# Normalising the softmax weights on POOL, and the small parts of the streamed weights on DVE, in a two-layer diffusion backbone

## The chip, the cores and the metric

One core of one Trainium2 chip runs the whole program in one launch. The metric is the device time of the launch in microseconds (us), lower is better. A difference under about 0.3% (6.4 us here) can't be told from no change.

The engines are named as the profile names them: PE (TensorE, matmuls and transposes), PEld (its weight loads), DVE (VectorE), ACT (ScalarE), POOL (GpSimd) and SP (SyncE, which here does nothing but issue DMAs; its issuing time stands under SPq). Each engine works through its own instructions in program order; engines wait for each other by semaphores. All tensors live in SBUF tiles of 128 partitions; matmul results come out in PSUM tiles of 128x512.

## The reference, cut to what matters

Two layers over 256 latent tokens (a grid of 4 rows by 64) and 256 context tokens, width 1024, fp32. A layer is a SwiGLU half step, a mixer and another SwiGLU half step. The change lies in the mixer, whose three branches are a neighbourhood attention (8 heads of 64), a Fourier mixing and a windowed attention (8 query heads, 2 key heads, a sink logit per head). Layer 0 also attends from the context tokens; layer 1, the last, doesn't.

```python
def neighbourhood_attention(q, k, v, kc, vc, bias_tab, rows):
    ...
    s_loc = jnp.where(in_win[:, :, None, :], s_loc, NEG_INF)
    ...
    p = jax.nn.softmax(jnp.concatenate([s_loc, s_ctx], axis=-1), axis=-1).astype(v.dtype)
    ...
def window_gqa_attention(q, k, v, kc, vc, sink):
    ...
    p = jax.nn.softmax(jnp.concatenate([s_loc, s_ctx, s_sink], axis=-1), axis=-1).astype(v.dtype)
    ...
def reference(...):
    h, hc = x, ctx
    for l in range(DEPTH):
        ...
        nq, nk, nv, fu, wq, wk, wv, gl = split_projection(u @ w_in[l])
        ...
        h = h + gt2 * merge_branches(a, f, w, gl, w_br[l], w_out[l])
```

## The kernel before

**The streamed weights.** Every projection runs over weights that come from HBM in 424 sub-tiles of 128x1024 (512 KB each, eight 128x128 blocks). The class `Weights` (L43 to L101) streams them. A product keeps fp32 accuracy by three matmuls per block, in `mm3` (L292 to L297): large part of the weight with large and small part of the activations (L295, L296), small part of the weight with the large part (L297). So each raw sub-tile is loaded by SP (L58), copied to its large part `wh` by ACT (L67), and its small part `wl` = raw minus `wh` is made at L76 by the engine in `lo_engine`. That engine is DVE, except at a few stretches where it is POOL; the two attention stretches (set by two lines in `mix`, L1056 and L1058) hold 18 sub-tiles in layer 0 and 22 in layer 1. `next` hands out the blocks. At the first block of sub-tile n it issues what is still missing of the `wl` of n, the `wh` of n+1 and the loads; at the fifth block the `wl` of n+1. The pool of raw tiles has 3 buffers, and a load waits until the `wl` three sub-tiles before has read its buffer.

**The attention.** 16 blocks in layer 0 and 8 in layer 1 (a block is a pair of heads over 256 queries) run through a software pipeline written out in `attention` (L720 to L848), with four steps per block. Step by step: two score matmuls (L733, L734) give a 128x512 tile of scores (128x256 for context queries). DVE adds the mask and takes the row's extreme (L740), ACT takes the exponential and its sum (L742; L745 for the sink). `normalise` takes two tiles at a time, tiles 0 and 1 of the block and two steps later tiles 2 and 3: DVE adds the sinks (L753), takes the reciprocals (L755) and scales both tiles (L759). Then PE transposes the weights chunk by chunk over all four tiles (L764), ACT copies the large part (L766), DVE makes the small part (L771), and PE multiplies with the values (L782). At a block's end ACT copies the result out (L788) and POOL adds its halves (`gather`, L794). Between the steps `fill` runs pieces of the projections that are due (queries, keys, gates) by a table of due times, `DUES`. It is these pieces that pull weights through `next`.

**The other users of the queues.** Projected keys and queries are stacked into operand tiles by DMAs from SBUF to SBUF that SP issues (`stack`, L891): four for a query, eight for a key. SP also issues the raw loads (L58) and the loads of the bias table (L714), all in program order. The rotary embedding runs on POOL (L913), and its small part is made on DVE (L918); `turn` copies the projected values on ACT (L935) and transposes them on PE (L939).

**The tiles.** Activations, scores and temporaries share one pool, `act_p`, of N_ACT tiles of 128x512. A tile's next writer waits for the last reader of what it held before, DMAs included.

Of the kernel before, what the change touches and what calls it, by code (L numbers as in the profile page):

```python
# [10 lines left out]
ALU = mybir.AluOpType  # L11
# [20 lines left out]
NEG = -1e30  # L32
SUB = 8
N_SUB = 424
N_ACT = 70
TAIL = 3
FOLD = (1, 2, 3)
EARLY_GATES = 6, 12
# [4 lines left out]
class Weights:  # L43


    def __init__(self, nc, src, raw_p, w_p):
        self.nc, self.src, self.raw_p, self.w_p = nc, src, raw_p, w_p
        self.order, self.pos = [], 0
        self.loaded = self.n_hi = self.n_lo = 0
        self.raw, self.hi, self.lo = {}, {}, {}  # L50
        self.on_tile = None
        self.lo_engine = nc.vector
        self.ahead = 1
# [30 lines left out]
    def next(self, key, width=1):  # L84
        n, o = divmod(self.pos, SUB)
        assert o + width <= SUB
        if o == 0:
            self.hi.pop(n - 1, None)
            self.lo.pop(n - 1, None)
            self.lo_to(n + 1)  # L90
            self.hi_to(n + 1 + self.ahead)
            self.load_to(self.n_lo + 3)
        elif o == SUB // 2:
            self.lo_to(n + 1 + self.ahead)
        if self.on_tile and o % self.tile_step == 2:
            self.on_tile()
        self.order.append((key, width))
        self.pos += width
        s = slice(o * 128, (o + width) * 128)
        return self.hi[n][:, s], self.lo[n][:, s]  # L100
# [165 lines left out]
class Emit:  # L266
    def __init__(self, ctx, tc, d):
        self.tc, self.nc, self.d = tc, tc.nc, d
        pool = lambda name, bufs, **k: ctx.enter_context(tc.tile_pool(name=name, bufs=bufs, **k))
        self.const = pool("const", 1)  # L270
        self.act_p = pool("act", N_ACT)
        self.raw_p = pool("raw", 3)
        self.w_p = pool("w", 6)
        self.mod_p = pool("mod", 2)
        self.sm_p = pool("sm", 4)
        self.ps_p = pool("ps", 8, space=PSUM)
        self.W = Weights(self.nc, d["ws"], self.raw_p, self.w_p)
        self.mod = {}
# [90 lines left out]
    def setup(self):  # L369
# [15 lines left out]
        self.first_w = {}  # L385
        loads = self.first_loads(0), self.first_loads(1)
        next(loads[0])
        self.h = [c.tile([128, NT], F32, name=f"h{k}") for k in range(KD)]
        for k in range(KD):
# [18 lines left out]
        for _ in range(KD // 2):  # L408
            next(scale)
        for k in range(KD):  # L410
            self.stat(k, 0, NT, True)
        norm = Norm(self, 0, 0, NT, self.first_shift)
        next(scale, None)
        norm.stage1(0, 1)
        self.first_shift(0)
# [304 lines left out]
    def attention(self, makers, fill):  # L720
# [3 lines left out]
        nc = self.nc  # L724
# [23 lines left out]
        def normalise(b, i0, i1):  # L748

            nk = len(b["kc"]) * 128  # L750
            r, s = b["r"][:, i0:i1], b["sum"][:, i0:i1]
            if b["sink"] is not None:
                nc.vector.tensor_tensor(out=s, in0=s, in1=b["es"][:, i0:i1], op=ALU.add)  # L753
                yield
            nc.vector.reciprocal(out=r, in_=s)  # L755
            yield
            for i in range(i0, i1):
                e = b["p"][i][:, :nk]
                nc.vector.tensor_scalar(out=e, in0=e, scalar1=b["r"][:, i:i + 1], scalar2=None, op0=ALU.mult)  # L759

        def transposes(b, c):
            ps = self.ps()
# [44 lines left out]
        for g in range(4 * len(makers) + 8):  # L807
            if g % 4 == 0 and g // 4 < len(makers):
                b = makers[g // 4]()
# [7 lines left out]
            for i in range(2):  # L817
                y = at(g, 3 + 2 * i, 1)
                if y:
                    norms.append(normalise(y[0], 2 * i, 2 * i + 2))  # L820
# [13 lines left out]
            for i in range(max(0, g // 4 - 4), len(blocks)):  # L834
                b = blocks[i]
# [15 lines left out]
    def mix(self, l, norm, nxt):  # L851
        nc, W = self.nc, self.W
# [200 lines left out]
        fill(0.0)  # L1053
        pieces(4)
        f = next(fourier)
        W.lo_engine = nc.gpsimd  # L1056
        self.attention(makers, fill)
        W.lo_engine = nc.vector  # L1058
        while pending or later:
            pieces(1, True)  # L1060
        early = [ready(("gate", i)) for i in range(n_early)]
# [175 lines left out]
```

## Time and profile before

| | us |
|---|---|
| median of 3 runs | 2136.06 |
| lowest and highest | 2133.22 and 2138.77 |
| the profiled execution | 2132.6 |
| its span, first to last instruction | 2130.8 |
| PE busy | 2058.0 (97%) |
| DVE busy | 1310.0 (61%) |
| ACT busy | 853.6 (40%) |
| POOL busy | 436.4 (20%) |

The busy share of an engine is an average over the whole span, in which the stages differ. The attention of layer 0 lies at about 500 to 680 us, that of layer 1 at about 1690 to 1840 us. In a row of the waits, the first name is the instruction that waited, the arrow points to what released it, and then stand total us, times, and the longest. In a row of the timeline the columns are start, length, engine, line, operation, tiles written and read, shape and count, and in brackets how long the engine sat idle before it and what ended that.

### The profile page before, as it was taken

To read this page: it belongs to the slowest core of one execution; us is meant where nothing else is said; L and a number is where in the kernel's file an instruction comes from. 1 tells how busy PE (TensorE), PEld (TensorE's weight loads), DVE (VectorE), ACT (ScalarE), POOL (GpSimd) and SP (SyncE) were. 2 spreads that over 40 slices of the span, in tenths; PEclk is the share of its full clock that TensorE was granted. 3 is DMA by queue.
4 is the path that set the end of the run, shared out by engine and by line. 5 is a ranking of instruction groups with operands and counts; after the bars stand their busy time and mean duration, and the time that the engine had idled before them with its cause. 6 is when DMAs were issued, how large, how long until landed. Compare 5 with 4: busy or idle time off the path is not lost. (4 is left out here: it accounts for less than half of the span.)

```text
span 2130.8 us, 29228 instructions
## 1 busy us (share of the span) xinstructions
PE 2058.0 (97%) x11193; PEld 1771.7 (83%) x11193; DVE 1310.0 (61%) x2074; ACT 853.6 (40%) x1362; POOL 436.4 (20%) x318
## 2 busy tenths in 40 slices
PE   7899999999999999999999999999999989999998
PEld 3788888878888888888888888888888878999998
DVE  6777776565676334777777575533337548566554
ACT  4422222345787223432222243222324458645443
POOL 4200000433542112600000140000024155332002
PEclk8999999999999999999999999999999999999999
DMA  6455556445522323455656545623334563555664
GB/s 250 138 198 187 192 194 212 138 120 151 137 82 80 96 93 99 134 181 192 195 187 201 198 145 189 195 92 99 99 116 139 145 170 113 150 179 157 182 183 131
DMA packets 119412, 327.05 MB, mean 153 GB/s; under 512 B 30692, under 2 KB 35940, under 8 KB 119272
## 3 DMA queue, kind: packets, MB, share of 16 engines
q1 hardware_dynamic: 119272, 325.18, 49.0%
q8 instruction: 88, 1.44, 0.3%
q14 instruction: 52, 0.43, 0.1%
HBM read 305.99 MB, written 1.05 MB: 144 GB/s over the span
## 5 line engine op out<-in xcount | busy, mean ns | idle before, releaser
L296 PE MATMUL ps<-act,wh 128*128 128x512 f32 (+1 forms) x3227 | 1122.3, 348 | 23.8 <-DVE act L220 11.7
L295 PE MATMUL ps<-act,wh 128*128 128x512 f32 (+1 forms) x3227 | 1122.8, 348 | 2.1 <-ACT act L208 1.1
L297 PE MATMUL ps<-act,wl 128*128 128x512 f32 (+1 forms) x3227 | 1120.6, 347 | 0.8 <-DVE wl L76 0.8
L67 ACT ACTIVATE wh<-raw 128x1024 fp32r<-128x1024 f32 x424 | 447.5, 1057 | 749.7 <-PE ps L296 596.6
L296 PEld LDWEIGHTS ps<-act,wh 128*128 128x128 f32 x3227 | 614.6, 190 | 100.5 <-DVE act L220 14.2
L295 PEld LDWEIGHTS ps<-act,wh 128*128 128x128 f32 x3227 | 614.5, 190 | 77.8 <-ACT act L208 1.3
L297 PEld LDWEIGHTS ps<-act,wl 128*128 128x128 f32 x3227 | 614.6, 190 | 76.2 <-DVE wl L76 1.1
L76 DVE TENSOR_TENSOR wl<-raw,wh 128x1024 fp32r<-128x1024 f32 x346 | 432.9, 1253 | 254.7 <-ACT wh L67 254.3
L317 DVE CUSTOM_DVE_ANT_0 dump<-ada,silu_row 128x1024 bf16<-128x1024 f32 x224 | 273.5, 1221 | 11.4 <-DMA ada<-in_w_ada 9.1
L76 POOL TENSOR_TENSOR wl<-raw,wh 128x1024 fp32r<-128x1024 f32 x78 | 190.9, 2450 | 239.4 <-ACT wh L67 226.2
L304 ACT ACTIVATE act<-tmp 128x512 fp32r<-128x512 f32 (+1 forms) x122 | 66.8, 566 | 268.5 <-DVE tmp L522 255.0
L460 POOL TENSOR_TENSOR tmp<-h 128x512 f32<-128x512 f32 (+1 forms) x7 | 11.6, 1660 | 737.0 <-DVE h L477 592.7
L477 DVE SCALAR_TENSOR_TENSOR h<-ps,mod,h 128x256 f32<-128x256 f32 x136 | 61.7, 481 | 150.9 <-PE ps L297 150.9
L522 DVE TENSOR_TENSOR tmp<-tmp,ps 128x512 f32<-128x512 f32 (+1 forms) x88 | 54.6, 621 | 113.6 <-PE ps L297 107.7
L305 DVE TENSOR_TENSOR act<-tmp,act 128x512 fp32r<-128x512 f32 (+1 forms) x122 | 74.3, 626 | 61.2 <-ACT act L304 61.2
L771 DVE TENSOR_TENSOR act<-ps,act 128x512 fp32r<-128x512 f32 x80 | 54.9, 686 | 33.5 <-ACT act L766 33.2
L466 POOL TENSOR_TENSOR tmp<-h 128x256 f32<-128x256 f32 (+1 forms) x44 | 51.6, 1174 | 116.3 <-DVE h L477 98.4
L742 ACT ACTIVATE tmp<-tmp,sm 128x512 f32<-128x512 f32 (+1 forms) x96 | 62.1, 647 | 29.1 <-DVE sm L740 27.4
L782 PE MATMUL ps<-act 128*128 128x256 f32 x320 | 63.1, 310 | 9.2 <-DVE act L771 8.0
L450 POOL MEMSET tmp<- 128x256 f32 x16 | 4.8, 312 | 308.5 <-PE ps L297 307.8
L766 ACT ACTIVATE act<-ps 128x512 fp32r<-128x512 f32 x80 | 47.5, 593 | 36.4 <-PE ps L764 35.9
L1101 DVE TENSOR_TENSOR tmp<-tmp,ps 128x512 f32<-128x512 f32 (+1 forms) x48 | 26.0, 551 | 54.3 <-PE ps L297 53.0
(111 smaller groups left out, 1479.5 us busy)
## 6 DMA issues: line engine op xcount, KB each, us to landing
raw<-in_ws SPq DMA_DIRECT2D x424, 512.0 KB, 3.7
ada<-in_w_ada SPq DMA_DIRECT2D x128, 512.0 KB, 3.7
act<-act SPq DMA_DIRECT2D x112, 128.0 KB, 2.3
tmp<-in_w_ada_sc SPq DMA_DIRECT2D x16, 256.0 KB, 5.4
tmp<-in_w_ada SPq DMA_DIRECT2D x16, 256.0 KB, 6.0
tmp<-in_na_bias SPq DMA_DIRECT2D x64, 64.0 KB, 2.7
h<-in_h SPq DMA_DIRECT2D x8, 256.0 KB, 5.6
act<-act SPq DMA_DIRECT2D x32, 64.0 KB, 2.0
```

The lines of the kernel that those rows point to most:

```text
L67: self.nc.scalar.activation(out=wh, in_=self.raw[i], func=AF.Copy)
L76: self.lo_engine.tensor_tensor(out=wl, in0=self.raw.pop(i), in1=self.hi[i].bitcast(F32), op=ALU.subtract)
L295: mm(ps, lhsT=w[0], rhs=x[0], start=start, stop=False)
L296: mm(ps, lhsT=w[0], rhs=x[1], start=False, stop=False)
L297: mm(ps, lhsT=w[1], rhs=x[0], start=False, stop=stop)
L304: nc.scalar.activation(out=hi, in_=src, func=AF.Copy)
L305: nc.vector.tensor_tensor(out=lo, in0=src, in1=hi.bitcast(F32), op=ALU.subtract)
L317: self.nc.vector.tensor_tensor_reduce(out=self.dump[:, ks], in0=w, in1=self.silu_row[:, v, ks], scale=1.0, scalar=m if half else 0.0, op0= ...
L477: self.nc.vector.scalar_tensor_tensor(out=h, in0=ps, scalar=self.mod[l, g][:, v, j:j + 1], in1=h, op0=ALU.mult, op1=ALU.add)
L742: nc.scalar.activation(out=e[:, :nk], in_=e[:, :nk], func=AF.Exp, scale=-1.0, bias=nm, accum_out=b["sum"][:, i:i + 1])
L771: nc.vector.tensor_tensor(out=t[1], in0=ps, in1=t[0].bitcast(F32), op=ALU.subtract)
L782: nc.tensor.matmul(b["ps"][hp][:, :256], lhsT=v, rhs=t[j][:, cs], start=c == 0 and j == 0, stop=c == n - 1 and j == 1)
```

## The change

`normalise` scales on POOL instead of DVE: 64 operations on 128x512 and 32 on 128x256 in all. The two assignments of `lo_engine` around the attention go, so 40 of the small parts are made on DVE that were made on POOL. The raw pool has 5 buffers for 3, and `next` issues the loads two sub-tiles further ahead. The pool of activation tiles has 66 tiles for 70.

```diff
-N_ACT = 70
+N_ACT = 66
...
-            self.load_to(self.n_lo + 3)
+            self.load_to(self.n_lo + 5)
...
-        self.raw_p = pool("raw", 3)
+        self.raw_p = pool("raw", 5)
...
             for i in range(i0, i1):
                 e = b["p"][i][:, :nk]
-                nc.vector.tensor_scalar(out=e, in0=e, scalar1=b["r"][:, i:i + 1], scalar2=None, op0=ALU.mult)
+                nc.gpsimd.tensor_scalar(out=e, in0=e, scalar1=b["r"][:, i:i + 1], scalar2=None, op0=ALU.mult)
...
         f = next(fourier)
-        W.lo_engine = nc.gpsimd
         self.attention(makers, fill)
-        W.lo_engine = nc.vector
```

Three places show how the instructions move. The first is POOL in the windowed attention of layer 0. Before, between the rotary products (L913) and the sums at a block's end (L794) stand small parts of weights (L76):

```order
L913 TENSOR_TENSOR tmp<-tmp,cos 128x256
L913 TENSOR_TENSOR tmp<-tmp,sin 128x256
L913 TENSOR_TENSOR tmp<-tmp 128x256
L794 TENSOR_TENSOR tmp<-tmp 128x256
L76 TENSOR_TENSOR wl<-raw,wh 128x1024
L794 TENSOR_TENSOR tmp<-tmp 128x256
L76 TENSOR_TENSOR wl<-raw,wh 128x1024
```

In the changed kernel the same place holds the scalings (L759), each pair behind one of the sums:

```order
L913 TENSOR_TENSOR tmp<-tmp,cos 128x256
L913 TENSOR_TENSOR tmp<-tmp,sin 128x256
L913 TENSOR_TENSOR tmp<-tmp 128x256
L794 TENSOR_TENSOR tmp<-tmp 128x256
L759 TENSOR_SCALAR tmp<-tmp,sm 128x512 x2
L794 TENSOR_TENSOR tmp<-tmp 128x256
L759 TENSOR_SCALAR tmp<-tmp,sm 128x512 x2
L759 TENSOR_SCALAR tmp<-tmp,sm 128x256 x4
```

The small parts have left POOL, and the second pair of scalings of a latent block now stands behind an L794.

The second place is DVE in the same stretch, around the small part of a rotated query (L918) and the small part of the transposed softmax weights (L771). Before:

```order
L755 RECIPROCAL sm<-sm 128x2
L759 TENSOR_SCALAR tmp<-tmp,sm 128x512 x2
L740 ISA tmp,sm<-ps,wa_mask,nsink 128x512
L740 ISA sm 128x1
L918 SCALAR_TENSOR_TENSOR act<-tmp,act 128x512
L771 TENSOR_TENSOR act<-ps,act 128x512
L740 ISA tmp,sm<-ps,wa_mask,nsink 128x256
```

And in the changed kernel:

```order
L755 RECIPROCAL sm<-sm 128x2
L740 ISA tmp,sm<-ps,wa_mask,nsink 128x512
L740 ISA sm 128x1
L918 SCALAR_TENSOR_TENSOR act<-tmp,act 128x512
L76 TENSOR_TENSOR wl<-raw,wh 128x1024
L771 TENSOR_TENSOR act<-ps,act 128x512
L740 ISA tmp,sm<-ps,wa_mask,nsink 128x256
```

A small part of weights (L76) now stands between L918 and L771, and the two scalings ahead of L740 are gone.

The third place is DVE in layer 1, where the last keys and queries of the neighbourhood attention are evacuated (L898). The names in brackets are semaphores that the instruction waits for; those that begin with DMA belong to transfers. Before:

```order
L898 SCALAR_TENSOR_TENSOR act<-ps,act 128x256 [waits DMAHW3_49,Activation_49]
L755 RECIPROCAL sm<-sm 128x2
L771 TENSOR_TENSOR act<-ps,act 128x512 [waits DMAHW2_49,DMAHW1_49,DMAHW3_49,DMAHW0_49,PE_49]
L759 TENSOR_SCALAR tmp<-tmp,sm 128x512 [waits DVE_49]
L759 TENSOR_SCALAR tmp<-tmp,sm 128x512
L740 ISA tmp,sm<-ps,tmp 128x512 [waits DMAHW0_49,DMAHW5_49,PE_49,Pool_49]
```

And in the changed kernel, from the same L898:

```order
L898 SCALAR_TENSOR_TENSOR act<-ps,act 128x256 [waits DMAHW0_49,DMAHW1_49,DVE_49,Activation_49]
L76 TENSOR_TENSOR wl<-raw,wh 128x1024 [waits Activation_49]
L76 TENSOR_TENSOR wl<-raw,wh 128x1024 [waits DVE_49,DMAHW5_49,PE_49,Activation_49]
L76 TENSOR_TENSOR wl<-raw,wh 128x1024 [waits DVE_49,DMAHW6_49,PE_49,Activation_49]
L755 RECIPROCAL sm<-sm 128x2
L771 TENSOR_TENSOR act<-ps,act 128x512 [waits DMAHW2_49,DMAHW3_49,DMAHW1_49,DMAHW0_49]
L740 ISA tmp,sm<-ps,tmp 128x512 [waits DMAHW4_49,DMAHW5_49,DVE_49,DMAHW7_49,PE_49,Pool_49]
```

Three small parts stand between L898 and L771 now. With 66 tiles for 70, L898, L771 and L740 write tiles that other transfers have read than before: in the changed kernel's program, L898 takes the tile that the last of the four moves issued from 1711.81 us reads, L771 one that the fifth to the eighth of the twelve moves issued from 1715.88 us read, and L740 one that the last of these twelve reads.

## Rows read from the trace of the kernel before

**Rows 1.** The busy times by stretch. Columns: the stretch in us from the span's start and its length, then the busy us of PE, PEld, DVE, ACT and POOL with the count of instructions, PE's mean granted clock as a share of full speed, the DMA engines' busy share and GB/s.

```profile
500.00:680.00 180.00, 174.37 (x969) 147.63 (x968) 123.85 (x311) 134.44 (x328) 73.85 (x60) 1.00 0.40 105
1723.00:1730.50 7.50, 0.36 (x4) 0.15 (x2) 0.91 (x3) 2.73 (x5) 2.66 (x2) 0.66 0.88 276
1730.50:1737.00 6.50, 6.50 (x31) 5.88 (x31) 0.87 (x3) 2.63 (x5) 5.72 (x6) 0.60 0.54 124
```

**Rows 2.** The waits between 500 and 680 us (attention of layer 0), those of PE.

```profile
PE ps L782 <- DVE act L771: 2.2, 7, 0.3
PE ps L733 <- DMA act<-act: 2.2, 1, 2.2
```

**Rows 3.** The waits between 1700 and 1840 us (attention of layer 1), those of ACT for raw weights and the longest of PE.

```profile
ACT wh L67 <- DMA raw<-in_ws: 19.1, 4, 8.6
PE ps L939 <- ACT tmp L935: 7.1, 1, 7.1
PE ps L782 <- DVE act L771: 5.8, 6, 1.9
```

**Rows 4.** The timeline of layer 1 around 1710 to 1731 us: ACT, PE, SP, DVE.

```profile
1720.44 1.06 ACT L67 ACTIVATE wh<-raw 128x1024 fp32r<-128x1024 f32 x1 [8.64 <-DMA raw<-in_ws]
1729.10 0.71 ACT L742 ACTIVATE tmp<-tmp,sm 128x512 f32<-128x512 f32 x1
...
1722.58 0.72 PE L782 MATMUL ps<-act 128*128 128x256 f32 x4
1730.44 0.90 PE L939 MATMUL ps<-ident,tmp 128*128 128x128 f32 x3 [7.14 <-ACT tmp L935]
...
1711.81 2.47 SPq L891 DMA_DIRECT2D act<-act  x4
1715.88 7.78 SPq L891 DMA_DIRECT2D act<-act  x12
...
1710.89 0.42 DVE L898 SCALAR_TENSOR_TENSOR act<-ps,act 128x256 fp32r<-128x256 f32 x1 [1.20 <-ACT act L896]
1722.52 0.69 DVE L740 CUSTOM_DVE_ANT_0 tmp<-ps,tmp 128x512 f32<-128x512 f32 x1 [7.56 <-PE ps L734]
```

**Rows 5.** The page's list of DMA issues: the moves from tile to tile, with the median us from issue to landing at the end of the row.

```profile
act<-act SPq DMA_DIRECT2D x112, 128.0 KB, 2.3
```

**Rows 6.** Groups of instructions on POOL over the whole span: after the shape the count, then busy us and mean ns of one, then the idle time before them.

```profile
L450 POOL MEMSET tmp<- 128x256 f32 x16 | 4.8, 312 | 308.5 <-PE ps L297 307.8
L441 POOL TENSOR_SCALAR nsink<-sink 128x32 f32<-128x32 f32 x1 | 0.3, 339 | 0.0
```

**Rows 7.** All operations of three lines over the whole span: count, shortest, median and longest in ns, first and last start, shapes. L1104 adds two tiles, L76 makes a small part of weights, L753 adds the sinks.

```profile
L1104 POOL TENSOR_TENSOR tmp<-tmp x14: 735/1292/2207, 679.2 to 1892.9; 128x512 f32<-128x512 f32 x7, 128x256 f32<-128x256 f32 x7
...
L76 DVE TENSOR_TENSOR wl<-raw,wh x346: 1212/1223/2335, 83.2 to 2113.3; 128x1024 fp32r<-128x1024 f32 x173
L76 POOL TENSOR_TENSOR wl<-raw,wh x78: 2342/2401/2900, 24.4 to 1940.4; 128x1024 fp32r<-128x1024 f32 x78
...
L753 DVE TENSOR_TENSOR sm<-sm x24: 148/156/1773, 593.3 to 1810.7; 128x2 f32<-128x2 f32 x24
```

**Rows 8.** The scalings L759 of 128x512, first those between 500 and 680 us, then those between 1720 and 1840 us.

```profile
L759 DVE TENSOR_SCALAR tmp<-tmp,sm 128x512 f32<-128x512 f32 x32 | 18.9, 634 | 0.5
...
L759 DVE TENSOR_SCALAR tmp<-tmp,sm 128x512 f32<-128x512 f32 x26 | 18.9, 766 | 0.3
```

**Rows 9.** The timeline at five places in the attention of layer 0: first POOL's operation behind which the second pair of scalings of a block stands in the changed order, then PE's four transposes (L764) of that block's first chunk.

```profile
580.76 0.80 POOL L913 TENSOR_TENSOR tmp<-tmp 128x256 f32<-128x256 f32 x1
582.21 0.60 PE L764 MATMUL ps<-ident,tmp 128*128 128x128 f32 x4
...
600.94 0.74 POOL L794 TENSOR_TENSOR tmp<-tmp 128x256 f32<-128x256 f32 x1 [1.12 <-ACT tmp L788]
601.92 0.60 PE L764 MATMUL ps<-ident,tmp 128*128 128x128 f32 x4
...
620.68 0.74 POOL L794 TENSOR_TENSOR tmp<-tmp 128x256 f32<-128x256 f32 x1 [1.11 <-ACT tmp L788]
621.69 0.60 PE L764 MATMUL ps<-ident,tmp 128*128 128x128 f32 x4
...
640.71 0.73 POOL L794 TENSOR_TENSOR tmp<-tmp 128x256 f32<-128x256 f32 x1 [1.72 <-ACT tmp L788]
640.18 0.93 PE L764 MATMUL ps<-ident,tmp 128*128 128x128 f32 x4
...
657.29 0.81 POOL L794 TENSOR_TENSOR tmp<-tmp 128x256 f32<-128x256 f32 x1 [0.92 <-ACT tmp L788]
657.61 0.60 PE L764 MATMUL ps<-ident,tmp 128*128 128x128 f32 x4
```

**Rows 10.** The timeline at two places in the attention of layer 0: DVE around 597 us with PE's L782 behind it, and the pair of scalings on DVE at 504.53 us.

```profile
596.87 0.69 DVE L918 SCALAR_TENSOR_TENSOR act<-tmp,act 128x512 fp32r<-128x512 f32 x1 [0.65 <-ACT act L916]
597.49 0.69 DVE L771 TENSOR_TENSOR act<-ps,act 128x512 fp32r<-128x512 f32 x1
598.50 1.34 DVE L753 TENSOR_TENSOR sm<-sm 128x2 f32<-128x2 f32 x1
...
598.24 0.62 PE L782 MATMUL ps<-act 128*128 128x256 f32 x3 [0.33 <-DVE act L771]
...
504.53 2.16 DVE L759 TENSOR_SCALAR tmp<-tmp,sm 128x512 f32<-128x512 f32 x2
```

## The prediction

> **What bounds the kernel now.** I read the busy shares first, then the windows, the waits, and last the timeline around the waits that count. PE is busy 97% of the span, so the time is PE's work plus the little that it waits; the change leaves PE's work as it is and can only add or remove waits. The windows show where they are [rows 1]. In the attention of layer 0 (180 us) PE is idle for 5.6 us. [...]
>
> The waits name the releasers. In layer 0 PE waits seven times for the small part of the transposed weights, L771, 2.2 us in all, and once for a transfer between tiles, 2.2 us [rows 2]. In layer 1 it waits 5.8 us for L771, and the one wait of 7.1 us for ACT's L935 is the hole [rows 3]. ACT itself had waited there for raw weights, 19.1 us in four waits. The timeline gives the chain [rows 4]: ACT gets its raw tiles late (8.64 us idle before 1720.44), and what is queued behind them, the exponential L742 at 1729.10 and L935 after it, releases PE's L939 only at 1730.44. SP is late as well: it issues four moves from 1711.81 and twelve from 1715.88, at about 0.65 us each. A move lands 2.3 us after its issue [rows 5].
>
> **The change part by part.**
>
> *The price of a scaling on POOL.* No row shows a 128x512 scaling there. Bounds: POOL's fill of 256 columns, which reads nothing, takes 0.312 us and a scaling of 32 columns 0.339 [rows 6]; POOL's sums of two inputs take 0.735 at the least (256 columns) and 1.292 in the middle of both widths, which is the short end of 512; a `wl` of 1024 takes 2.40 [rows 7]. From 512 to 1024 columns that is (2401 − 1292)/512 = 2.17 ns a column, with 0.18 us fixed. The fill by the same fixed part has (312 − 180)/256 = 0.5 ns. One input halfway between none and two gives 1.34 ns, so 0.18 + 0.69 = 0.87, rounded to 0.9 us. Ends: 0.34 and 1.29.
>
> [...]
>
> *Term A: scalings that come too late for PE.* On DVE 32 scalings of 128x512 took 18.9 us in layer 0, beside PE's work [rows 8]. On POOL a pair takes 1.8 us and is queued behind an L794 or L913, as the order of the changed kernel shows. A block's second pair has one step to be ready, and PE's third transpose, which reads it, starts 0.2 us into the group. I compared the end of the POOL operation ahead, plus 0.1 of passing on, plus 1.8, with PE's need at all blocks; five places in layer 0 come out late [rows 9]. First: 580.76 + 0.80 + 1.9 = 583.46 for 582.41, so 1.05. Second: 603.58 for 602.12, 1.46. Third: 623.32 for 621.89, 1.43. Fourth (PE's third transpose at 640.7, since the group is drawn out): 643.34, 2.64. Fifth: 660.00 for 657.81, 2.19. PE goes in order and nothing stands by to fill, so the sum, **+8.8 us**, is on the path. The small parts that leave POOL don't bring these L794 forward: ACT's L788 releases four of them after 0.9 to 1.7 us of idle time. With 0.34 the sum is 3.2, with 1.29 it is 12.7.
>
> *Term B: small parts on DVE.* Each takes 1.22 us there [rows 7], and where L771 stands behind it PE gets that late. At 598.24 PE starts L782 after 0.33 us of waiting for L771, which ran straight behind L918 [rows 10]. In the new order a `wl` stands between the two; that L918 had waited for ACT, so the absent scalings give nothing back. Two more of the seven waits (618 and 655 us) have the same order. 3 × 1.22 = **+3.7**. At the other four nothing comes between and DVE has two scalings fewer: at most their part of the waits goes, 2.2 × 4/7 = **−1.3**. The transfer that PE waited 2.2 us for begins behind the pair of scalings at 504.53 (2.16 us), which a `wl` of 1.22 replaces: **−0.9**. The price of 1.22 holds if POOL doesn't hold DVE up; the slowest `wl` took 2.34.
>
> *Term C: the hole in layer 1.* Loads two sub-tiles ahead end ACT's waits for raw tiles. What is late next is a tile. With 66 of them L898 (at 1710.89 in the timeline) writes one that the four moves from 1711.81 read, the last issued by 1714.28: landed at about 1716.5. DVE goes in order, so three `wl` and L771 stand behind. L771 also writes a tile that the fifth to eighth of the twelve moves read: 1715.88 + 8 × 0.65 = 1721.1, landed at 1723.4, while PE wants it at 1722.58. The last of the twelve is issued by 1723.66 and lands at about 1726.0; L740, which writes its tile, takes 0.7, ACT may have a large part in hand (1.06, as at 1720.44), and from the exponential's start to PE's L939 it took 1.34 (1729.10 to 1730.44). PE's L939 would start at about 1729.1 for 1730.44: **−1.3**, with the half clock as before. If no transfer held, the wait and the clock's loss would go together: −7.1 − 2.6 = −9.7. If transfers land 1 to 2 us later (beside raw loads that are now sooner), nothing is won.
>
> *The rest.* In layer 1's later attention 26 scalings of 0.766 us leave DVE, 19 us [rows 8], and `wl` come in their place at 1.22 each (the 22 of the stretch, less those before 1720); POOL loses them at 2.4 and gets the scalings at 0.9. L771's waits there (5.8) may go up or down by 2.5; I take 0. Outside the attention the loads are hidden anyway: ACT's raw waits in the list are those of the hole, and SP's place for each load is the same program point, so earlier loads give 0 there; 5 for 3 buffers cost nothing but the tiles.
>
> **Sum:** 8.8 + 3.7 − 1.3 − 0.9 − 1.3 = +9.0 on the profiled execution of 2132.6. That lies 3.5 us under the median, and the prediction is of the median: 2136.06 + 9.0 = **2145**.
>
> **The rivals.**
>
> *R1, the hole goes wholly.* The twelve moves are ready earlier because the projections before them aren't held by raw tiles, so SP and its tiles catch up. For it: ACT idled 19.1 us for four raw tiles. Against it: SP's queue is long by its own issuing (16 moves of about 0.65), whatever the weights do. Then −9.7 for −1.3: +0.6, 2136.7, no change.
>
> *R2, the other side: DVE is relieved where PE waits.* If a pair of scalings costs 1.2 us or less on POOL (0.62 each), A is 6.0 or less; with the hole gone (−9.7) and DVE free of scalings in time, the waits for L771 go in both layers (−2.2 and −5.8), and the three `wl` of term B slip into DVE's idle time. 6.0 − 9.7 − 8.0 = −11.7: 2124. It decides from about 0.6 us a scaling and with the moves landed before 1722. For it: DVE idles 31% of the layer-0 stretch [rows 1]. Against it: DVE's work is in order, and the `wl` are pulled in exactly where L918 and L771 follow each other.
>
> *R3, POOL and DVE hold each other up.* L753 on two columns takes 0.156 us in the middle, but up to 1.77 [rows 7], and at 598.50, beside a `wl` on POOL, 1.34 [rows 10]. If scalings on POOL suffer from DVE's `wl` in the same way, a scaling costs 1.29 (A is 12.7), nothing is relieved, three pairs more have L753 held for 3 × (1.34 − 0.156) = 3.5, and the longer hole loses another 2.6 to the clock: 12.7 + 3.7 + 3.5 + 2.6 = +22.5, 2158.6. Against it: the two-input work on POOL, which was there when L753 was slow, is what leaves.
>
> [...]
>
> **How the numbers follow.** Chances: the forecast 0.45, R1 0.20, R2 0.21, R3 0.14. The likeliest one's own range runs from +3.5 (scalings of 0.34) to +13 (1.29): 2139.5 to 2149. The range of 8 in 10 takes in R1, most of R2 and R3: 2124 to 2158. About 0.3% (6.4 us) is what a measurement can tell from no change. Faster: R2 and a little of R1, 0.24. Within: most of R1 and the forecast's lower edge, 0.26. Slower: 0.50.
>
> **What would show it.** Scalings of about 0.9 us in POOL's rows for L759; PE waits for POOL's L759 before L764 at five places near 581 to 658, 1 to 2.6 us each, about 9 in all; PE's wait for L771 near 598, 618 and 655 grown to about 1.5. In layer 1, no wait of ACT for raw tiles near 1711 to 1728, DVE idle behind a transfer at L898, and L939 at about the same distance behind the last L782 less 1 us. The prediction is wrong if scalings take under 0.5 us, if PE's idle time in the layer-0 attention stays near 5.6, or if the half clock behind the hole is gone.

## The result, and the profile after

The changed kernel takes 2160.22 us (median of 4 runs, 2158.01 to 2162.48) where the kernel before takes 2134.64 (median of 4). The ratio is 1.0122, with a 95% interval of 1.0104 to 1.0139: slower by 25.6 us. The forecast was 2145 with a range of 2124 to 2158: the direction was right, the size was too small, and the time lies above the range. The profiled execution has a span of 2157.8, 27.0 longer than the 2130.8 of before.

The page of the changed kernel, its busy times and the groups of the scalings and of the transposes behind them:

```profile
PE 2062.3 (96%) x11193; PEld 1772.9 (82%) x11193; DVE 1295.2 (60%) x2018; ACT 853.9 (40%) x1362; POOL 473.0 (22%) x374
...
L759 POOL TENSOR_SCALAR tmp<-tmp,sm 128x512 f32<-128x512 f32 (+1 forms) x96 | 132.7, 1395 | 191.6 <-DVE sm L755 126.7
...
L764 PE MATMUL ps<-ident,tmp 128*128 128x128 f32 x320 | 55.6, 286 | 26.5 <-POOL tmp L759 25.1
```

Over the whole program PE is busy 4.3 us longer for the same work, and its transposes wait 25.1 us for POOL's scalings, a wait that before did not exist. To see where, I took the moments at which the same score matmul (L733) starts in both traces. Before the attention of layer 0 the changed kernel is 2.4 us ahead (other kernels of this study enter it 0.2 to 2.4 us ahead too, so I read nothing into that); at the last L733 of layer 0 it is 24.9 behind, at the first of layer 1 25.4, ahead of the hole 27.0, behind it 23.5, at the end 27.0. So the attention of layer 0 alone loses 27.3 us, as much as the whole program; layer 1 wins 3.4 across the hole and loses 5.1 around it. The stretch of layer 0 from the first to the last L733, before and after, in the view by stretch (columns as in [rows 1]):

```profile
496.69:659.44 162.75, 157.46 (x874) 133.27 (x873) 113.08 (x293) 120.88 (x299) 69.90 (x57) 1.00 0.43 111
```

```profile
494.28:684.31 190.03, 167.62 (x874) 140.31 (x873) 99.40 (x251) 122.45 (x302) 110.62 (x102) 0.95 0.38 98
```

Two things come out of these rows. PE's idle time goes from 162.75 − 157.46 = 5.3 us to 190.03 − 167.62 = 22.4: +17.1. And the same 874 matmuls keep PE busy 10.2 us longer, for the granted clock is 0.95 and no longer 1.00. The waits of PE between 500 and 700 us in the changed kernel answer to [rows 2]:

```profile
PE ps L764 <- POOL tmp L759: 18.7, 15, 2.4
PE ps L782 <- DVE act L771: 3.9, 6, 1.4
```

The waits for the small part L771 grew by 1.7, the transfer that PE had waited 2.2 us for is gone from the list, and 18.7 us are new. The scalings on POOL, by shape:

```profile
L759 POOL TENSOR_SCALAR tmp<-tmp,sm 128x512 f32<-128x512 f32 x64 | 103.5, 1629 | 149.8 <-DVE sm L755 99.2 <-ACT act L896 50.6
...
L759 POOL TENSOR_SCALAR tmp<-tmp,sm 128x256 f32<-128x256 f32 x32 | 29.2, 926 | 41.8 <-DVE sm L755 27.5 <-PE ps L734 5.3 <-ACT sm L745 4.7
```

One takes 1.63 us in the mean on 512 columns, not 0.9. The first of the five places of [rows 9], POOL and then PE:

```profile
583.59 0.72 POOL L913 TENSOR_TENSOR tmp<-tmp 128x256 f32<-128x256 f32 x1
584.28 3.11 POOL L759 TENSOR_SCALAR tmp<-tmp,sm 128x512 f32<-128x512 f32 x2
...
585.90 0.33 PE L764 MATMUL ps<-ident,tmp 128*128 128x128 f32 x1 [2.00 <-POOL tmp L759]
587.45 0.47 PE L764 MATMUL ps<-ident,tmp 128*128 128x128 f32 x1 [1.21 <-POOL tmp L759]
```

PE's third transpose waits for the first scaling of the pair and its fourth for the second, 3.2 us in all. Right behind it, and behind four of the later waits, PE runs at half speed. Four of the five falls, by stretch:

```profile
586.30:592.50 6.20, 5.05 (x18) 4.48 (x19) 2.87 (x5) 3.18 (x8) 3.59 (x4) 0.51 0.34 78
613.50:617.00 3.50, 3.50 (x14) 3.02 (x13) 1.53 (x5) 1.07 (x4) 1.82 (x2) 0.53 0.00 0
637.60:641.00 3.40, 3.40 (x12) 2.82 (x12) 0.96 (x3) 1.79 (x5) 1.63 (x2) 0.50 0.00 0
661.50:665.00 3.50, 3.50 (x15) 3.20 (x14) 1.72 (x5) 2.34 (x8) 1.83 (x2) 0.52 0.02 5
```

The granted clock in these is 0.50 to 0.53 of full speed. Stretches of 1 us, each with its busy time times one minus its clock, add up to 9.1 us in layer 0; before, there was none.

In layer 1 the hole of [rows 3, 4] is smaller and has the new cause that was forecast. DVE and PE of the changed kernel around it:

```profile
1742.89 0.42 DVE L898 SCALAR_TENSOR_TENSOR act<-ps,act 128x256 fp32r<-128x256 f32 x1 [6.48 <-DMA act<-act]
1743.23 2.35 DVE L76 TENSOR_TENSOR wl<-raw,wh 128x1024 fp32r<-128x1024 f32 x2
1747.69 1.23 DVE L76 TENSOR_TENSOR wl<-raw,wh 128x1024 fp32r<-128x1024 f32 x1 [2.10 <-ACT wh L67]
1750.96 0.69 DVE L771 TENSOR_TENSOR act<-ps,act 128x512 fp32r<-128x512 f32 x1 [1.97 <-DMA act<-act]
...
1751.71 0.62 PE L782 MATMUL ps<-act 128*128 128x256 f32 x3 [1.80 <-DVE act L771]
1753.99 1.11 PE L939 MATMUL ps<-ident,tmp 128*128 128x128 f32 x4 [1.66 <-ACT tmp L935]
```

L898 waits 6.48 us for moves between tiles, three small parts stand behind it, L771 waits for another move, and PE pays 1.80 + 1.66 where it had paid 7.1.

### The profile page after: what moved, and what is told of

The parts are those of the page before. It is cut to its first block, busy times and chain, and to the rows that moved or that the text cites. A ratio compares the mean times of both kernels' runs of the same rounds, so it can differ in the third digit from the quotient of the medians.

```text
span 2157.8 us, 29369 instructions
## 1 busy us (share of the span) xinstructions
PE 2062.3 (96%) x11193; PEld 1772.9 (82%) x11193; DVE 1295.2 (60%) x2018; ACT 853.9 (40%) x1362; POOL 473.0 (22%) x374
## 5 line engine op out<-in xcount | busy, mean ns | idle before, releaser
L296 PEld LDWEIGHTS ps<-act,wh 128*128 128x128 f32 x3227 | 615.3, 191 | 103.9 <-DVE act L220 15.4
L76 DVE TENSOR_TENSOR wl<-raw,wh 128x1024 fp32r<-128x1024 f32 x386 | 482.7, 1252 | 259.3 <-ACT wh L67 258.8
L759 POOL TENSOR_SCALAR tmp<-tmp,sm 128x512 f32<-128x512 f32 (+1 forms) x96 | 132.7, 1395 | 191.6 <-DVE sm L755 126.7
L522 DVE TENSOR_TENSOR tmp<-tmp,ps 128x512 f32<-128x512 f32 (+1 forms) x88 | 54.6, 621 | 114.6 <-PE ps L297 108.3
L76 POOL TENSOR_TENSOR wl<-raw,wh 128x1024 fp32r<-128x1024 f32 x38 | 92.9, 2449 | 78.6 <-ACT wh L67 68.5
L771 DVE TENSOR_TENSOR act<-ps,act 128x512 fp32r<-128x512 f32 x80 | 54.9, 686 | 44.3 <-ACT act L766 42.2
L764 PE MATMUL ps<-ident,tmp 128*128 128x128 f32 x320 | 55.6, 286 | 26.5 <-POOL tmp L759 25.1
L764 PEld LDWEIGHTS ps<-ident,tmp 128*128 128x128 f32 x320 | 41.8, 146 | 39.8 <-POOL tmp L759 30.2
```

The source lines that it names most:

```text
L76: self.lo_engine.tensor_tensor(out=wl, in0=self.raw.pop(i), in1=self.hi[i].bitcast(F32), op=ALU.subtract)
L296: mm(ps, lhsT=w[0], rhs=x[1], start=False, stop=False)
L759: nc.gpsimd.tensor_scalar(out=e, in0=e, scalar1=b["r"][:, i:i + 1], scalar2=None, op0=ALU.mult)
L764: nc.tensor.transpose(ps[:, i * 128:(i + 1) * 128], b["p"][i][:, c * 128:(c + 1) * 128], self.ident)
L771: nc.vector.tensor_tensor(out=t[1], in0=ps, in1=t[0].bitcast(F32), op=ALU.subtract)
```

## The experiments

Three theories stood against each other: late scalings on POOL, small parts on DVE that hold up L771, and fewer tiles that bring waits for transfers. Four kernels take the change apart.

**Only the scalings on POOL** (from the kernel before):

```diff
-                nc.vector.tensor_scalar(out=e, in0=e, scalar1=b["r"][:, i:i + 1], scalar2=None, op0=ALU.mult)
+                nc.gpsimd.tensor_scalar(out=e, in0=e, scalar1=b["r"][:, i:i + 1], scalar2=None, op0=ALU.mult)
```

> Only the scalings move to POOL; the small parts of the weights stay on POOL in the attention, 3 raw buffers, 70 tiles. Late scalings (theory 1): they are the cause by themselves, so the attention of layer 0 is at least as slow as in the changed kernel (PE waits for L759 18.7 us or more there, and its clock falls to half behind the longer waits); since POOL has the small parts at 2.4 us each beside them, more: 2160 to 2200 us. Small parts on DVE (theory 2): without them the loss is gone, under 2145 us. Fewer tiles (theory 3): under 2145 us as well.

Measured: 2180.8 us, a ratio of 1.0203 (1.0186 to 1.0219). PE's waits in the attention of layer 0 (490 to 720 us):

```profile
PE ps L764 <- POOL tmp L759: 24.5, 13, 3.7
PE ps L782 <- DVE act L771: 1.3, 4, 0.3
```

In layer 1 (1700 to 1870 us) another 15.7 us of waits for L759 come; the changed kernel has 6.3 there. Alone, the scalings lose 45 us; that the small parts leave POOL in the changed kernel gives back a part of it.

**Only the small parts on DVE** (from the kernel before):

```diff
-        W.lo_engine = nc.gpsimd
         self.attention(makers, fill)
-        W.lo_engine = nc.vector
```

> Only the 40 small parts move to DVE; the scalings stay there too. Late scalings: nothing of the loss, 2125 to 2142 us; PE's waits for L771 in the attention of layer 0 grow from 2.2 to about 4 to 6 us. Small parts on DVE: at least half of the loss, 2147 us or more. Fewer tiles: no loss, near 2135 us.

Measured: 2143.07 us, 1.0040 (1.0026 to 1.0054). That is 8 us slower, a little above what the first theory allowed and below the second's. In layer 0 PE's waits for L771 are 5.3 us as expected. The rest is in layer 1, whose waits (1685 to 1860 us) have a new longest one:

```profile
PE ps L782 <- DVE act L771: 16.8, 10, 8.0
PE ps L939 <- ACT tmp L935: 1.7, 1, 1.7
```

With 3 raw buffers the hole only moves: ACT still waits 15.8 us for raw tiles, DVE's small parts wait for ACT, and L771 is queued behind them, so PE loses 8.0 us one wait earlier.

**Only the loads: 5 raw buffers, loads two ahead, 66 tiles** (from the kernel before):

```diff
-N_ACT = 70
+N_ACT = 66
-            self.load_to(self.n_lo + 3)
+            self.load_to(self.n_lo + 5)
-        self.raw_p = pool("raw", 3)
+        self.raw_p = pool("raw", 5)
```

> Only the 5 raw buffers, the loads two ahead and the 66 tiles. Late scalings: no loss, 2128 to 2140 us; the hole in layer 1 (7.1 us before L939) shorter by 1 to 7 us with a wait for a transfer in its place. Small parts on DVE: near 2135 us. Fewer tiles: 10 us of the loss or more, 2145 us or above.

Measured: 2131.02 us, 0.9976 (0.9965 to 0.9987): 4 us faster than the kernel before, about the size of what can be told. L939 waits 2.8 us for 7.1, and L898 7.6 us for a transfer in the place of ACT's waits for raw tiles. L771 waits 6.0 us for another transfer, and PE's waits for L771 there are 7.8 us for 5.8; the 66 tiles cost nothing else that shows.

**The changed kernel with the scalings back on DVE** (the first diff undone in it).

> The changed kernel with the scalings back on DVE. Late scalings: the whole loss goes, 2125 to 2140 us, PE's clock at 1.00 through the attention of layer 0. Small parts on DVE: most of the loss stays, or more, as DVE then has both: above 2150 us. Fewer tiles: above 2145 us.

Measured: 2137.68 us, 1.0009 (0.9994 to 1.0024): no change against the kernel before. So 2160.22 − 2137.68 = 22.5 of the 25.6 us hang on the engine of the scalings alone. The clock in layer 0 was 0.99, not quite the 1.00 expected, behind a wait of 4.5 us for a transfer.

Five more ask why the scalings cost so much: by coming late, by their length, or by POOL and DVE holding each other up.

**The second pair of a block back on DVE** (from the changed kernel, as the next ones):

```diff
-                nc.gpsimd.tensor_scalar(out=e, ...)
+                (nc.gpsimd if i0 == 0 else nc.vector).tensor_scalar(out=e, ...)
```

> The changed kernel with a block's second pair of scalings back on DVE; the first pair stays on POOL. Late scalings: the first pair has two steps more (about 5 us) for its 3.1 us, so PE's waits for POOL's L759 go from 18.7 us to under 2 in the attention of layer 0, its clock stays at 1.00, and the time is 2125 to 2142 us. Rival, POOL and DVE hold each other up wherever the scalings stand: half of the scalings still on POOL keep half of the loss, 2147 to 2152 us.

Measured: 2133.41 us, 0.9990 (0.9980 to 0.9999). Half of the scalings are on POOL still and none of the loss is left. In the same stretch of layer 0 PE is idle for 8.5 us, and the clock is at 1.00 throughout:

```profile
495.19:661.54 166.35, 157.90 (x874) 133.43 (x873) 114.34 (x280) 120.57 (x301) 76.57 (x71) 1.00 0.44 112
```

No wait of PE for POOL's scalings is left in either layer. The first pair has two steps more, and takes 1.68 us a scaling with no harm. It is the due time, not POOL's share, that decides.

**Tiles 0 and 2 back on DVE, 1 and 3 on POOL:**

```diff
-                nc.gpsimd.tensor_scalar(out=e, ...)
+                (nc.gpsimd if i % 2 else nc.vector).tensor_scalar(out=e, ...)
```

> The changed kernel with every second scaling (tiles 0 and 2) back on DVE, so a pair costs one scaling of 1.57 us on POOL for two. Late scalings: each block's wait of 1.6, 0.6, 2.4, 3.2, 2.2, 2.2, 3.6, 3.0 us falls by up to 1.57, leaving about 7 of 18.7, and most of the five falls of the clock go: 2138 to 2150 us. Rival, POOL and DVE hold each other up: half of the loss stays, 2147 to 2152 us, with scalings of more than 1.6 us.

Measured: 2136.08 us, 1.0001 (0.9992 to 1.0011): the waits for L759 in layer 0 are 4.9 us in five places for 18.7 in fifteen, the clock there 0.99. One scaling less in each pair took 24 us off, and the time is 2 us below the range.

**The scaling as a product of two inputs:**

```diff
-                nc.gpsimd.tensor_scalar(out=e, in0=e, scalar1=b["r"][:, i:i + 1], scalar2=None, op0=ALU.mult)
+                nc.gpsimd.tensor_tensor(out=e, in0=e, in1=b["r"][:, i:i + 1].to_broadcast([128, nk]), op=ALU.mult)
```

> The changed kernel with the scaling on POOL written as a product of two inputs (the weights and the reciprocal read again for every column). If the price lies in the form of the operation, 1.29 us for 1.57 as the sums at L1104 had: 0.55 us less for a pair, 4.4 us less waiting over the eight blocks of layer 0 and some of the clock's loss, 2150 to 2157 us. If two inputs hold DVE up, or the repeated read costs more, L759 is 1.57 or above and the time 2158 us or more.

Measured: 2142.59 us, 1.0033 (1.0021 to 1.0046), 17.6 us less than the changed kernel and better than either answer had it. The same work on the same engine is shorter by a third, by shape:

```profile
L759 POOL TENSOR_TENSOR tmp<-tmp,sm 128x512 f32<-128x512 f32 x64 | 70.0, 1114 | 156.5 <-DVE sm L755 106.0 <-ACT act L896 50.5
...
L759 POOL TENSOR_TENSOR tmp<-tmp,sm 128x256 f32<-128x256 f32 x32 | 19.5, 630 | 42.1 <-DVE sm L755 32.6 <-PE ps L734 3.9 <-PE ps L764 3.3
```

Its waits in layer 0 are 5.7 us. The length of a scaling sets the loss, which is the same theory from its other side.

**The scaling by a constant** in place of each row's reciprocal:

```diff
-                nc.gpsimd.tensor_scalar(out=e, in0=e, scalar1=b["r"][:, i:i + 1], scalar2=None, op0=ALU.mult)
+                nc.gpsimd.tensor_scalar(out=e, in0=e, scalar1=0.25, scalar2=None, op0=ALU.mult)
```

> The changed kernel with the scaling on POOL by a constant for the reciprocal of each row, so the weights leave unnormalised (by 0.25 for all rows). If reading the scalar of each partition makes the price, a scaling of 512 falls from 1.57 us to 1.1 or less; if it is the scaling operation itself, it stays at 1.5 to 1.6 and the time at 2157 to 2163 us.

Measured, in one run: 2148.42 us. The length hardly changed, so it is the scaling operation and not the scalar of each partition that is slow:

```profile
L759 POOL TENSOR_SCALAR tmp<-tmp 128x512 f32<-128x512 f32 x64 | 98.4, 1553 | 117.9 <-ACT tmp L742 114.0 <-DVE act L771 2.2 <-DMA act<-act 1.7
```

I had missed that the time would fall all the same. The row suggests why: POOL now waits for the exponential (L742) and no more for DVE's reciprocal (L755), so the pair can start sooner. PE's waits for it in layer 0 fall to 11.7 us.

**PE kept busy in the wait:**

```diff
             for i in range(4):
+                if i == 2 and c == 0 and len(blocks[1]["kc"]) == 2 and len(b["kc"]) == 4:
+                    for _ in range(16):
+                        nc.tensor.transpose(ps[:, 256:384], self.ident, self.ident)
                 nc.tensor.transpose(...)
```

> The changed kernel with 16 transposes of the identity on PE ahead of the third transpose of the first chunk in the eight latent blocks of layer 0, about 1.75 us that lies in the wait; their result is written over. If it is PE's idling there that brings its clock to half, the clock stays at 1.00 in this stretch and most of the 9.1 us that half speed cost come back, less about 1.5 for the two blocks that wait shorter than that: 2150 to 2156 us. If the clock falls for another reason: 2159 to 2164 us, with the five falls as before.

Measured: 2154.99 us, 1.0090 (1.0075 to 1.0105), 5.2 us less than the changed kernel with 128 transposes more. The stretch of layer 0:

```profile
495.09:677.60 182.51, 172.23 (x1003) 147.29 (x1002) 99.19 (x250) 121.47 (x302) 111.24 (x101) 1.00 0.39 102
```

The clock is at 1.00 throughout, and the stretch is 7.5 us shorter than the 190.03 of the changed kernel. So what PE did before its clock fell was to idle in the waits for L759; with work there it didn't fall.

Three last kernels looked for a version that is faster still.

**The first pair on POOL as a product of two inputs, the second on DVE, in the changed kernel** (e10), **and the same with the small parts left on POOL** (e11, made from the kernel with 5 raw buffers):

```diff
+                if i0 == 0:
+                    nc.gpsimd.tensor_tensor(out=e, in0=e, in1=b["r"][:, i:i + 1].to_broadcast([128, nk]), op=ALU.mult)
+                else:
+                    nc.vector.tensor_scalar(out=e, in0=e, scalar1=b["r"][:, i:i + 1], scalar2=None, op0=ALU.mult)
```

> Small parts on DVE, 5 raw buffers, 66 tiles, the first pair of a block scaled on POOL by the product of two inputs, the second on DVE. Late scalings: no wait for POOL's L759; the time is that of the kernel with the second pair on DVE, 2133, less up to 3: 2129 to 2136 us. If the two-input products hold up DVE's small parts: 2137 us or more.

Measured: 2139.59 us, 1.0023 (1.0012 to 1.0034). No wait for POOL is left, and yet it is 6 us slower than with the scaling form on POOL. Against that kernel PE's waits for the small part L771 (the added lines make it L774) are longer by 1.7 and 1.3 us in the two layers, and in the two attentions it loses 3.3 us more to the clock. For layer 0 the trace gives the cause, and it is the second answer's: two small parts of weights stand between L918 and L771 there, and beside a pair of products on POOL each takes 2.06 us. The first of them, and the same place with the scaling form on POOL (the second pair on DVE):

```profile
595.84 2.06 DVE L76 TENSOR_TENSOR wl<-raw,wh 128x1024 fp32r<-128x1024 f32 x1
...
595.32 3.48 POOL L760 TENSOR_TENSOR tmp<-tmp,sm 128x512 f32<-128x512 f32 x2
...
596.26 1.22 DVE L76 TENSOR_TENSOR wl<-raw,wh 128x1024 fp32r<-128x1024 f32 x1
...
595.76 4.86 POOL L759 TENSOR_SCALAR tmp<-tmp,sm 128x512 f32<-128x512 f32 x2
```

PE's two waits behind them go from 1.45 and 1.17 us to 2.30 and 1.98, which is the whole 1.7. Why L771 is later in layer 1 stays open.

> The small parts stay on POOL, 5 raw buffers, 66 tiles, the first pair of a block scaled on POOL by the product of two inputs, the second on DVE. POOL has both then: where a first pair stands behind a small part of 2.4 us it is 2 x 1.11 + 2.4 = 4.6 us, just inside the two steps of about 5 us. If that suffices: 2128 to 2134 us, PE's waits for L771 below 2.2 us in layer 0. If not, PE waits for POOL's L759 again, with a few us: 2134 to 2142 us.

Measured: 2140.79 us, 1.0027 (1.0015 to 1.0039). The time is in the second answer's range, but not by its cause: PE waits for no scaling on POOL but 3.9 us for those on DVE. Beside POOL's small parts and products DVE's sum of the sinks and its scalings take far longer (the added lines make L762 the scaling on DVE):

```profile
L762 DVE TENSOR_SCALAR tmp<-tmp,sm 128x512 f32<-128x512 f32 x32 | 34.5, 1120 | 0.5
...
L753 DVE TENSOR_TENSOR sm<-sm 128x2 f32<-128x2 f32 x24 | 17.9, 747 | 2.1 <-ACT sm L745 2.1
```

In e10, without the small parts on POOL, these are 0.647 and 0.219 us.

**4 raw buffers, loads one further ahead, 68 tiles, nothing else** (from the kernel before; the third diff with 68, 4 and 4).

> Scalings and small parts as before; 4 raw buffers, the loads one further ahead, 68 tiles. If the hole in layer 1 comes from raw tiles alone, it shrinks as with 5 and the wait of L898 for a transfer that 66 tiles brought goes: 2127 to 2132 us. If one load further ahead isn't enough, ACT still waits for raw tiles near the hole: 2132 to 2136 us.

Measured: 2129.88 us, 0.9975 (0.9966 to 0.9985), the fastest of all and 4.5 us under the kernel before. The hole is down to a wait of 1.6 us for L935 (1690 to 1860 us):

```profile
PE ps L782 <- DVE act L771: 8.2, 8, 3.2
PE ps L764 <- ACT tmp L907: 1.8, 1, 1.8
PE ps L939 <- ACT tmp L935: 1.6, 1, 1.6
```

L898 waits for ACT only, as in the kernel before; L771 still waits 5.6 us for a move between tiles. Against the kernel with 5 buffers (2131.02) the difference can't be told.

## Why the prediction was right or wrong

**The price of a scaling on POOL: wrong, and the step that failed.** I put one input "halfway between none and two" and rounded to 0.9 us, between 0.34 and 1.29. It takes 1.57 us wherever nothing holds it (58 of the 64 take 1.555 to 1.575; at 606.50 us, beside an idle DVE, 1.569), outside both ends. The upper end of 1.29 was the short end of the sums of 512 columns, and not the dearest of them. The row by shape of the same sums in the trace before:

```profile
L1104 POOL TENSOR_TENSOR tmp<-tmp 128x512 f32<-128x512 f32 x7 | 11.7, 1673 | 127.1 <-DVE tmp L1101 106.6 <-ACT wh L67 20.5
```

Four of the seven took 1.29 and three 2.14 to 2.21, so the mean is 1.67. But a higher end would only have covered the price by luck, for the price doesn't follow the number of inputs, which is where the working failed: the product of two inputs takes 1.04 in the middle of cases (1.114 in the mean), the scaling with one 1.57. From 256 to 512 columns the scaling adds (1.567 − 0.927)/256 = 2.5 ns a column, the product (1.042 − 0.615)/256 = 1.7.

**Term A: the mechanism right, mis-sized.** PE waits for L759 ahead of L764 as said, the third transpose for the first scaling and the fourth for the second. With 1.57 in the same working the five places would have given 15.4 us for 8.8. They measured 3.2, 2.2, 2.2, 3.6 and 3.0: 14.2. What the short price had hidden is that the three earlier latent blocks come out late as well, with 1.6, 0.6 and 2.4 us. Together 18.7. Both experiments that shorten the pair (2136 and 2143 us) and the one that gives it time (2133) confirm it. The 0.1 of passing on was my estimate; in the changed kernel PE starts 0.05 to 0.06 us after the scaling that it waited for.

**Missing from the sum: the clock.** The sum had waits at their own length. Behind five of them PE ran at half speed, 9 to 10 us more. With it the stretch of layer 0 adds up: 18.7 + 1.7 − 2.2 + 9 to 10 = 27 to 28, for 27.3 measured. The fall was in view in the trace before: behind the hole PE was busy for 6.5 us at a mean granted clock of 0.60 [rows 1], which cost 6.5 × (1 − 0.60) = 2.6 us and is the half clock of term C; in stretches of 1 us the clock there was 0.50 from 1730 to 1735 us. I carried it for that hole alone and not for the waits that the change adds. The kernel that keeps PE busy, with its clock at 1.00 in that stretch, shows that here the idling brings it.

**Term B: the mechanism right at two of its three places, the third misread.** The forecast was +3.7, −1.3 and −0.9, together +1.5 for layer 0; measured are +1.7 for PE's waits for L771 and −2.2 for the transfer, whose wait went altogether: −0.5. Where a small part came between L918 and L771 PE waits 1.45 us (for 0.33 at 598) and 1.17 (at 618, where the trace before lists no wait):

```profile
605.83 0.62 PE L782 MATMUL ps<-act 128*128 128x256 f32 x3 [1.45 <-DVE act L771]
630.83 0.62 PE L782 MATMUL ps<-act 128*128 128x256 f32 x3 [1.17 <-DVE act L771]
```

The prediction counted 618 and 655 among the seven waits of [rows 2], but these lie at 580, 585, 598, 627, 638, 644 and 671 us. At 655 L771 had waited for ACT, with no L918 ahead of it:

```profile
653.85 0.69 DVE L771 TENSOR_TENSOR act<-ps,act 128x512 fp32r<-128x512 f32 x1 [0.55 <-ACT act L766]
```

At that place of the changed kernel (674 us) PE waits no longer than before. Three of the other waits (585, 627, 644) went, 0.9 us. By themselves the small parts on DVE lose 4.8 us in that stretch (167.54 for 162.75).

**Term C: the mechanism right, the gain larger.** ACT's waits for raw tiles went, L898 waited for the moves (6.48 us), L771 for another, as read from the tiles. −3.4 us across the hole for −1.3 forecast: the moves landed soon enough for PE to be only 3.5 us late. The half clock behind it was still there, as said, but for less time: at 1753.7 to 1757.1 us it is 0.50, which costs 1.6 us for the 2.6 before. The rest of layer 1 was put at 0 ± 2.5 and lost 5.1, 1.6 ahead of the hole and 3.5 behind it. The waits for L759 there (6.3 us) are the largest new item.

**The rivals.** R1 and R2 had the hole gone wholly, which didn't happen; R2 asked for a scaling of 0.62 as well. R3's time, 2158.6, is the nearest, but not its cause. The trace of the changed kernel has scalings that take longer beside work on DVE, but only at a few places: two scalings of layer 0 took 3.07 us, both begun beside DVE's L918 with a small part behind it. POOL and DVE at one of them:

```profile
603.45 4.62 POOL L759 TENSOR_SCALAR tmp<-tmp,sm 128x512 f32<-128x512 f32 x2
...
603.35 0.69 DVE L918 SCALAR_TENSOR_TENSOR act<-tmp,act 128x512 fp32r<-128x512 f32 x1 [0.82 <-ACT act L916]
603.96 1.22 DVE L76 TENSOR_TENSOR wl<-raw,wh 128x1024 fp32r<-128x1024 f32 x1
```

4.62 for a pair is 1.5 us more than twice 1.57. This was a first pair, and PE didn't wait for it. Mostly nothing was held: of the 14 small parts in the two attentions that DVE began while a scaling ran on POOL, 12 took 1.21 to 1.24 us, as did the 296 in the whole trace with nothing on POOL beside them (1.21 to 1.23), and 59 of the 64 scalings were within 0.1 us of 1.57, where R3 had scalings suffer from DVE's small parts. One of the small parts, and the pair beside it:

```profile
1777.09 3.10 POOL L759 TENSOR_SCALAR tmp<-tmp,sm 128x512 f32<-128x512 f32 x2
...
1779.18 1.22 DVE L76 TENSOR_TENSOR wl<-raw,wh 128x1024 fp32r<-128x1024 f32 x1
```

L753, which should have been held three times more by R3, came down from a mean of 0.430 us to 0.208.

**By parts, from the runs:** loads and tiles −4.3 (2131.02 against 2135.29), small parts on DVE +6.7 on top of them (2137.68 − 2131.02), scalings on POOL +22.5 on top of both. Together they make 24.9 of the 25.6, which were measured against other runs of the kernel before.

## What to carry to other kernels

Price a moved operation by a row of the same operation, shape and engine, and where there is none leave the upper end above the neighbours: on POOL a scaling of one input takes longer (1.57 us) than the shortest sum of two (1.29). A step that is handed to a slower engine costs what it is late for its reader, so hand over the half that has slack (here a block's first pair) and keep the half that is due. And where a trace shows PE's clock fall behind one idle stretch, a sum over new waits of PE should carry the chance of such a fall, not their own length alone.

## What the runs showed of the hardware

On POOL a 128x512 fp32 scaling takes 1.57 us in the middle of cases with a scalar for each partition (1.63 in the mean) and 1.49 with a constant (1.55), but the product with the same scalar read as a second input 1.04 (1.11). In the kernel before four of seven sums of two tiles of that shape take 1.29. DVE's scalings of 512 columns go from 0.717 us (mean) to 0.591 when the small parts beside them on POOL are gone (the fourth kernel against the kernel before); in the kernel before those that began with nothing running on POOL took 0.47 to 0.49, and the longest, begun beside a small part on POOL, 2.67. At one place in the order (a pair on POOL begun beside L918, with a small part behind that) the scaling on POOL took 3.07 us for 1.57, and the small part 1.22 as elsewhere; with the product on POOL the small part took 2.06. And in the eight latent blocks of layer 0 five waits (2.2 to 3.6 us, each in two pieces) were followed by a granted clock of about 0.50 for 3 to 7 us, while three (0.6, 1.6 and 2.4 us) were not.
